# A two-layer diffusion transformer in split fp32 on one core: single chunk loads in the opening, one weighing step moved, and a new order at both joints of attention and MLP

## The chip, the core and the metric

The kernel runs on one core of one Trainium2 chip. A core has five engines that run side by side and are tied by semaphores: TensorE (PE in the profile) multiplies and transposes, VectorE (DVE), ScalarE (ACT) and GpSimd (POOL) work element by element, and SyncE (SP) issues most of the transfers from HBM. The metric is device time in microseconds, lower is better. Times in the profile count from the start of the span, that is from the first instruction of the profiled execution.

## The reference

One image (256 tokens, width 1024) and one context (256 tokens) go through two blocks. Each block scales and shifts its input by a vector made from a conditioning vector (`ada_w`), mixes the tokens, adds the gated result, normalises, and does the same with an MLP. The first block's mixer is a retention in both directions with 4 heads, the second's a neighbourhood attention with 32 heads. The second block needs no output for the context. Cut to what matters here:

```
for i in range(2):
    mod = silu_c @ ada_w[i] + ada_b[i]; mod_c = silu_cc @ ada_w[i] + ada_b[i]
    sh1, sc1, g1, sh2, sc2, g2 = split(mod, 6)            # the same for mod_c
    h, hc = x * (1 + sc1) + sh1, ctx * (1 + sc1c) + sh1c
    y, yc = (retention_mixer, neighbourhood_mixer)[i](h, hc, ...)
    x = layer_norm(ALPHA * x + g1 * y)
    h = x * (1 + sc2) + sh2
    x = layer_norm(ALPHA * x + g2 * (relu(h @ w1[i]) ** 2 @ w2[i]))
    # i == 0: the same two steps for ctx with mod_c and yc
return x
```

In the retention, `finish` normalises each head's output, multiplies it by `silu(g)` and projects it with `w_o`.

## The kernel before

**Split numbers.** All large products run on fp32 numbers split in two: a high part (a cast to fp32r on ScalarE, tile names that end in `hi` or `h`) and a low part (what is left, a subtraction on VectorE, `lo` or `l`). A product is three matmuls: high by high, high by low, low by high (`mm3`, which keeps the three together). So each weight tile goes through four steps: `fetch` has SP load it into one of four `raw` buffers (512 KB), ScalarE casts `hi`, `lows` has VectorE subtract `lo`, and TensorE uses both. The `raw` buffer is free again when `lo` is done. SP issues its loads in program order, and each waits until its buffer is free. `take(n, ahead, open_)` fetches up to `ahead` units, makes their low parts, and hands out the next n; with `open_` that many of the low parts may still be outstanding.

**Order.** An engine's instructions are put in order by a scheduler of the framework, except where a flag on the engine's wrapper (`InOrder`, whose call is L84, so that nearly all rows of the profile carry that line) keeps them in program order: `pe.on`, `act.on`, `dve.on`, `pool.on`. SP is always in program order. At the places of the change the flags are on: the order there is written by hand. Each engine works its queue strictly from the front, so an instruction that waits holds up all behind it.

**Opening.** The first modulation, the queries and the values of head 0 are computed in eight chunks of 128 of the 1024 input columns. For each chunk SP loads modulation weights (`rawq`, two transfers), the columns of x and context (into `R`), and the weights of Q and V (`raw`). Chunks 0 and 1 are loaded singly (`chunk_loads`), the others in pairs with rows twice as long (`pair_loads`). TensorE then does `chunk_sums` (32 small matmuls, `pada`), `chunk_turn` (transposes of the tokens, `pt`), `chunk_columns`, and with the modulated tokens (`hTh`, `hTl`) the products of the queries (`chunk_q`, into `pq`) and of the values (into `pv`: `part_v` by parts for chunks 0 and 1, `chunk_v` token block by token block for the rest). `first_columns` and `first_biases` transpose the conditioning vector and the bias rows, which come by ScalarE's queue. `turn_over(n)` puts n matmuls on a constant tile (`still`) into TensorE's queue; their result is not used.

**First head.** After the projections of K and the gates, `masked_scores`, four outputs `po` (normalised into `on` and `gs`) and two `gates` calls follow. `to_oT(t)` transposes `gs` (into `pT`) and splits it into `oh` and `ol`; `tok` multiplies these by `w_o`. For t = 2, 3 `gs` needs `sg`, the silu of the last gates. Beside that runs a background: `bg()` does one step of `bg_stream`, which loads 512 KB of later modulation weights (`rawa`, into the same four buffers) and weighs them: the first nine steps are matmuls for the gate rows, the following ones are VectorE work (`weigh`, four operations on `strips` a step, in order), and every step issues the load of the next one.

**First joint**, from the last head of the retention to the first layer's MLP: per token block t a normalisation (`stat`, `moments`, `white` with `shift_of`), transposes (`turn`), scale and shift (`affine`) and split (`mod_split`). The first two pairs of hidden blocks are computed for the latent tokens (`LAT`) while the context's blocks 2 and 3 are still on their way, and then for the context (`CTX`), into the other half of the same banks. `evac1` takes the square of the relu out of a bank (`relu_sq`: `r`, then `hid`). Before the context half all flags of `ORDER` go off.

**Second joint**, from the neighbourhood attention to the second MLP: `gather`, `attend`, `invert`, `flip` and `turned` are the steps of the last score blocks (the result goes into `oTh`, `oTl`), `wo_first` and `wo_last` the two halves of the output projection (`pnw`), `settle_last` adds them, `center` and `mod_pt` make the normalised tokens and their transposes, and `tok_part` does single parts of the first products of the MLP (`p1t`) for token blocks 0 and 1. `activate` and `turn_block` make the first hidden block of them. The loop over `f4` then does the other hidden blocks with `mm1` in the usual form; its first pass is the `opening`.

Of the kernel before, what the change touches and what calls it, by code (L numbers as in the profile page):

```python
# [17 lines left out]
P = 128  # L18
# [86 lines left out]
def kernel(  # L105
# [171 lines left out]
    def lows(n=100):  # L277
        for lo, raw, hi in pending[:n]:
            dve.tensor_sub(out=lo, in0=raw, in1=hi.bitcast(F32))
        del pending[:n]  # L280
# [66 lines left out]
    def ln_columns(rows):  # L347
# [9 lines left out]
        pool.dma_start(out=lns[:], in_=lsc[0:64, :P])  # L357

# [400 lines left out]
    def chunk_ada(k):  # L759

        raw = slot(AQ[k], [P, 2, KC, P], F32, "rawq")
# [5 lines left out]
    def pair_ada(k):  # L767

        raws = []
        for kh in range(2):  # L770
            raw = slot(AQ[k % 4 + kh], [P, 2, 4, 2 * P], F32, "rawq")
            for i in range(2):
                w_ap = ada_w[0][512 * kh : 512 * kh + 512, i * D + P * k : i * D + P * k + 2 * P]
                sp.dma_start(out=raw[:, i], in_=w_ap.rearrange("(k p) n -> p k n", p=P))
            raws.append(raw)
        for j in range(2):
            adas[k + j] = lambda i, kk, j=j: raws[kk // 4][:, i, kk % 4, tsl(j)]

    def chunk_x(k, n=1):
        cols = slice(P * k, P * (k + n))  # L780
# [28 lines left out]

    def pair_loads(k):  # L810
        pair_ada(k)
        chunk_x(k, 2)
        for j in range(2):
            ws[k + j] = Weights(k + j)

    still = scr("still", F32R)
    dve.memset(still[:].bitcast(F32), 1.0)
# [114 lines left out]
    def chunk_v(k, ts):  # L934
        w = ws[k]
        for t in ts:
            mm3(
                pv[t][:], hs(k, t * P, (t + 1) * P), (w.hi[:, w.V], w.lo[:, w.V]), k == 0, k == KC - 1
            )

    def part_v(k, a, b):
        w, h = (ws[k].hi, ws[k].lo), hs(k, 0, NT)
        for t in range(4):
            pe.matmul(
                pv[t][:], lhsT=h[a][:, tsl(t)], rhs=w[b][:, Weights.V],
                start=(k == 0 and a == b), stop=False,
            )
# [18 lines left out]
    turn_over(5)  # L966
# [9 lines left out]
    for k in range(KC):  # L976
# [6 lines left out]
        if k == 1:  # L983
# [3 lines left out]
        elif k:  # L987
            chunk_q(k)
        if k < KC - 1:
# [5 lines left out]
            if k > 1:  # L995
                ws[k + 1].low()
        if k in (0, 2):
            pair_loads(k + 4)
        if k > 1:
            chunk_v(k, (0, 1))  # L1000
        else:
            part_v(k, 1, 0)
        if k < KC - 1:
            chunk_columns(k + 1)
            chunk_modulate(k + 1, lambda: None if k > 1 else ws[k + 1].low())
        if k > 1:
            chunk_v(k, (2, 3))
        else:
            part_v(k, 0, 1)
# [62 lines left out]
    for h in range(RH):  # L1072
# [34 lines left out]
        def gates(ts, between=()):  # L1107

            pgs = [bank("pg") for _ in ts]
            for k in range(KC):  # L1110
# [3 lines left out]
                if h == 0 and k % 4 == 3 and (k < 4 or len(ts) > 1):  # L1114
# [56 lines left out]
        for t in range(4):  # L1171
# [14 lines left out]
            if t < 2:  # L1186
                pool.tensor_mul(out=gs[:, t, :], in0=on, in1=gs[:, t, :])

# [42 lines left out]
        else:  # L1231
# [14 lines left out]
            def white(t, mv, r):  # L1246
                act.activation(out=xns[t], in_=R[t], func=AF.Identity, scale=r[:], bias=shift_of(mv, r)[:])
# [18 lines left out]
            white(0, *m0)  # L1266
# [8 lines left out]
            white(1, *m1)  # L1275
# [12 lines left out]
            white(2, *m2)  # L1288
# [27 lines left out]

    G2 = None
    for hf in range(2):
# [9 lines left out]
        if hf == 0:  # L1328
            us = take(2, 2)
# [27 lines left out]
        for fp in range(len(hid), 8):  # L1357
# [3 lines left out]
            mm1(us, ALL, pb)  # L1361
            dve.on = hf == 0
# [544 lines left out]
    def wo_last(t, half, cols=slice(0, 512)):  # L1907
        ps = wops[half, t, cols.start] if half else bank("pnw")
        mmo(ps, t, (4, 5, 6, 7), us[2 * half : 2 * half + 2], cols, start=half == 0)
        return ps  # L1910
# [33 lines left out]
    lows(1)  # L1944
# [8 lines left out]
    us4 = take(2, 0)  # L1953
# [65 lines left out]
    lo0 = [affine_half(pts0, half, 0, True, (dve, pool)[half]) for half in range(2)]  # L2019
# [3 lines left out]
    lo0[0]()  # L2023
# [3 lines left out]
    fetch(2)  # L2027
    us4 += take(2, 0, 2)
    lo0[1]()
    mv1, r1 = moments(1)  # L2030
    p00, p01 = [bank("p1t") for _ in range(2)]
# [6 lines left out]
    tok_part(p00, 0, 0, *HL, HIGH)  # L2038
    tok_part(p00, 0, 0, *LH, LOW)
    tok_part(p01, 0, 1, *HH, start=True)  # L2040
    tok_part(p01, 0, 1, *LH, LOW)
    tok_part(p00, 0, 0, *LH, HIGH, stop=True)
# [181 lines left out]
```

## Time and profile before

| | |
|---|---|
| median of 3 runs | 1200.78 us (1199.64 to 1201.06) |
| profiled execution | 1201.29 us, of which its span 1199.5 us |
| mean granted clock of TensorE | 0.997 |
| busy share of TensorE, VectorE, ScalarE, GpSimd | 98%, 69%, 40%, 21% |
| traffic of the span | 193.16 MB, mean 161 GB/s |
| opening (chunks, until K of head 0) | 0 to 64.4 us |
| first head's outputs and gates | about 100 to 127 us |
| first joint | about 433 to 470 us |
| second joint | about 976 to 1052 us |

A row of the timeline gives start, length, engine, line, operation, output from inputs, shape and count, and in brackets how long the engine was idle before it and what ended that. A row of a window gives its length, then busy time and count of TensorE, its weight loads, VectorE, ScalarE and GpSimd, the granted clock, the share of the transfer engines and GB/s. Matmuls are pipelined: the length of one in the timeline is longer than the distance to the next one's start, and the distance is what counts.

### The profile page before, as it was taken

Reading aid. Unit: us, or ns where it says so; the run is one execution under the profiler, and the core shown is the slowest. Engines: PE = TensorE matmul, PEld = TensorE weight load, DVE = VectorE, ACT = ScalarE, POOL = GpSimd, SP = SyncE. Lnnn points to the kernel's source line nnn. Section 1 sums busy time; section 2 is a strip of 40 time slices with the busy share of each in tenths; the row PEclk is TensorE's granted clock in tenths of the full one; section 3 lists DMA queues with packets and bytes.
Section 4 is the critical chain, followed back from the end, with each engine's and each line's share of the span. In section 5 each row is a group of like instructions: output and inputs, shape, how many; then the busy total and the mean of one; then the engine's idle time right before and its main releaser. Section 6 shows DMA issues by size and latency. Waiting matters only on the chain.

```text
span 1199.5 us, 17825 instructions
## 1 busy us (share of the span) xinstructions
PE 1176.4 (98%) x6867; PEld 987.8 (82%) x6867; DVE 832.7 (69%) x1307; ACT 477.6 (40%) x809; POOL 250.9 (21%) x390
## 2 busy tenths in 40 slices
PE   7999999999999999999999999999999999999997
PEld 5777788888888889888888888889788878999886
DVE  3784976787688477668766675578577588787446
ACT  3561222323222246442212432237466665556341
POOL 1102500310330141582203000123343431000001
PEclk9999999999999999999999999999999999999999
DMA  9774543344345124866566665656344435566760
GB/s 304 222 230 126 158 157 105 106 141 141 96 150 152 59 71 141 243 120 199 172 184 203 210 198 192 193 154 201 86 139 126 114 122 155 175 212 204 234 209 37
DMA packets 130265, 193.16 MB, mean 161 GB/s; under 512 B 9676, under 2 KB 73332, under 8 KB 130180
## 3 DMA queue, kind: packets, MB, share of 16 engines
q1 hardware_dynamic: 121796, 179.02, 47.8%
q0 software_dynamic: 7232, 10.44, 4.1%
q10 hardware_dynamic: 1152, 2.56, 0.8%
q8 instruction: 54, 0.88, 0.3%
q14 instruction: 31, 0.25, 0.1%
HBM read 187.15 MB, written 5.75 MB: 161 GB/s over the span
## 4 chain that ended last, share of the span: by engine, by line
PE 87%; DVE 7%; DMA 2%; ACT 2%; issue 2%; POOL 1%; DVEq 0%; ACTq 0%; POOLq 0%; SPq 0%
PE p L84 40%; PE pq L84 7%; PE pv L84 7%; PE pg L84 7%; PE pw L84 6%; PE pn L84 5%; PE pnv L84 4%; PE po L84 2%; DVE lo L84 2%; PE pada L84 2%; PE ppt L84 2%; PE pS L84 1%; PE pqk L84 1%; PE pav L84 1%; DMA raw<-in_mlp_w_dram 1%
## 5 line engine op out<-in xcount | busy, mean ns | idle before, releaser
L84 ACT CAST hi<-raw 128x1024 fp32r<-128x1024 f32 (+2 forms) x228 | 231.7, 1032 | 316.5 <-PE p L84 117.7
L84 DVE TENSOR_TENSOR lo<-raw,hi 128x1024 fp32r<-128x1024 f32 (+2 forms) x228 | 277.3, 1229 | 100.7 <-ACT hi L84 100.3
L84 PE MATMUL p<-hi,hid 128*128 128x512 f32 (+1 forms) x832 | 241.6, 373 | 0.0
L84 PEld LDWEIGHTS p<-hi,hid 128*128 128x128 f32 x832 | 152.1, 188 | 27.7
L84 PE MATMUL p<-hTh,lo 128*128 128x256 f32 (+1 forms) x512 | 167.4, 327 | 3.0 <-DVE lo L84 3.0
L84 PE MATMUL p<-hTh,hi 128*128 128x256 f32 (+1 forms) x512 | 167.8, 328 | 0.2 <-ACT hTh L84 0.2
L84 PE MATMUL p<-hTl,hi 128*128 128x256 f32 (+1 forms) x512 | 167.2, 327 | 0.3 <-DVE hTl L84 0.3
L84 PE MATMUL p<-lo,hid 128*128 128x512 f32 (+1 forms) x416 | 155.2, 373 | 0.0
L84 DVE SCALAR_TENSOR_TENSOR acc<-rawa,scol,acc 128x1024 f32<-128x1024 f32 x56 | 74.7, 1344 | 65.5 <-DMA rawa<-in_ada_w_dram 65.5
L84 PEld LDWEIGHTS p<-hTh,lo 128*128 128x128 f32 x512 | 96.4, 188 | 12.3 <-DVE lo L84 3.6
L84 PEld LDWEIGHTS p<-hTl,hi 128*128 128x128 f32 x512 | 96.4, 188 | 9.4 <-DVE hTl L84 0.8
L84 PEld LDWEIGHTS p<-hTh,hi 128*128 128x128 f32 x512 | 96.3, 188 | 9.2 <-ACT hTh L84 0.4
L84 POOL TENSOR_TENSOR R<-R,acc 128x512 f32<-128x512 f32 x40 | 60.3, 1521 | 205.2 <-DVE acc L84 204.9
L84 PEld LDWEIGHTS p<-lo,hid 128*128 128x128 f32 x416 | 78.4, 188 | 13.6
L84 ACT CAST hid<-r 128x256 fp32r<-128x256 f32 (+1 forms) x64 | 32.0, 500 | 112.4 <-DVE r L84 112.4
L84 DVE SCALAR_TENSOR_TENSOR strips<-rawa,scol,strips 128x512 f32<-128x512 f32 x84 | 64.3, 822 | 0.0
L84 POOL TENSOR_TENSOR rstd<-rstd,misc 128x1 f32<-128x1 f32 x28 | 18.8, 672 | 209.4 <-DVE rstd L84 208.1
L84 ACT ACTIVATE s<-s,mn 128x512 f32<-128x512 f32 x64 | 45.5, 712 | 26.2 <-DVE mn L84 26.2
L84 PE MATMUL pw<-hi,oh 128*128 128x512 f32 x128 | 51.6, 403 | 0.0
L84 PE MATMUL pg<-hi,hTh 128*128 128x512 f32 x128 | 51.3, 401 | 0.0
L84 PE MATMUL pw<-hi,ol 128*128 128x512 f32 x128 | 50.5, 395 | 0.5 <-DVE ol L84 0.5
L84 DVE TENSOR_TENSOR hid<-r,hid 128x256 fp32r<-128x256 f32 (+1 forms) x64 | 34.5, 539 | 23.0 <-ACT hid L84 22.9
(238 smaller groups left out, 2308.9 us busy)
## 6 DMA issues: line engine op xcount, KB each, us to landing
raw<-in_mlp_w_dram SPq DMA_DIRECT2D x128, 512.0 KB, 4.6
rawa<-in_ada_w_dram SPq DMA_DIRECT2D x80, 512.0 KB, 3.9
raw<-in_ret_w_in_dram SPq DMA_DIRECT2D x42, 512.0 KB, 3.7
raw<-in_nat_w_in_dram SPq DMA_DIRECT2D x24, 512.0 KB, 5.0
rawq<-in_ada_w_dram SPq DMA_DIRECT2D x16, 512.0 KB, 6.6
raw<-in_ret_w_o_dram SPq DMA_DIRECT2D x16, 512.0 KB, 3.8
bias<-rpb_rows POOLq DMA_DIRECT2D x32, 128.0 KB, 2.9
raw<-in_nat_w_o_dram SPq DMA_DIRECT2D x8, 512.0 KB, 5.2
```

Of the source, the lines that this page charges most:

```text
L84: r = f(*args, **kwargs)
```

## The change

Four places change; the computation stays the same.

1. Opening: all chunks are loaded singly, four ahead (`pair_loads` is gone). All chunks run by parts: high by high first, then the high weights by the low tokens. Fillers: 16 ahead of everything, then 3, 1, 3 and 4 where there were 5 and 5. The sums of chunk 0 stand ahead of the bias transpose.
2. First head: after the first output, `bg_until(9)` and one more step of the background; in `gates` only the call at k = 3 is left.
3. First joint: a unit is fetched earlier, with its low part separately; the split of blocks 2 and 3 is made as high part now and low part later (`mod_high`); the context half of the first two pairs is done with all high by high products first (`ctx_mm1`), and TensorE keeps program order through it, until the first `mm1` of the following loop.
4. Second joint: `invert(n)` moves behind `attend(n - 1)`, a fetch in separate rows moves behind `attend(n)`, the last projection goes by parts (`wo_parts`), low parts of weights move between the steps, the low part of the tokens' second half goes from GpSimd to VectorE, the first parts of the MLP get a new order, and in the loop's opening one fetch and one low part follow each `relu_sq`.

```
+    def mod_high(tmp, half, t):
+        ks = slice(4 * half, 4 * half + 4)
+        raw, hi, lo = tmp[:].rearrange("p (k t) -> p k t", k=4), hTh[:, ks, tsl(t)], hTl[:, ks, tsl(t)]
+        act.copy(out=hi, in_=raw)
+        return lambda: dve.tensor_sub(out=lo, in0=raw, in1=hi.bitcast(F32))
...
-    for k in range(2):
+    for k in range(4):
         chunk_loads(k)
-    pair_loads(2)
     for e in (act, dve, pe):
         e.on = True
+    turn_over(16)
     first_columns()
+    turn_over(3)
+    chunk_sums(0, 0)
+    chunk_row(0, tsl(0))
+    turn_over(1)
     first_biases()
-    chunk_sums(0, 0)
-    turn_over(5)
-    chunk_row(0, tsl(0))
+    turn_over(3)
     chunk_sums(0, 1)
...
-    turn_over(5)
+    turn_over(4)
...
-        if k == 1:
+        if k:
             chunk_q(k, ((0, 0),))
             part_v(k, 0, 0)
             chunk_q(k, ((1, 0), (0, 1)))
-        elif k:
-            chunk_q(k)
...
-        if k in (0, 2):
-            pair_loads(k + 4)
-        if k > 1:
-            chunk_v(k, (0, 1))
-        else:
-            part_v(k, 1, 0)
+        if k < 4:
+            chunk_loads(k + 4)
+        part_v(k, 1, 0)
...
-                if h == 0 and k % 4 == 3 and (k < 4 or len(ts) > 1):
+                if h == 0 and k == 3:
                     bg(2 if G1s[0] is None else 1)
                     first_gate()
...
+            if h == 0 and t == 0:
+                bg_until(9)
+                first_gate()
+                bg()
...
+    def ctx_mm1(us, pb):
+        for i in range(2):
+            for k in (4, 5, 6, 7, 0, 1, 2, 3):
+                pe.matmul(
+                    pb[i][:, CTX], lhsT=us[k // 4][0][:, k % 4, tsl(i)], rhs=hTh[:, k, CTX],
+                    start=k == 4, stop=False,
+                )
+        for i in range(2):
+            for k in (4, 5, 6, 7, 0, 1, 2, 3):
+                wh, wl = (w[:, k % 4, tsl(i)] for w in us[k // 4])
+                pe.matmul(pb[i][:, CTX], lhsT=wl, rhs=hTh[:, k, CTX], start=False, stop=False)
+                pe.matmul(pb[i][:, CTX], lhsT=wh, rhs=hTl[:, k, CTX], start=False, stop=k == 3)
...
-            us = take(2, 2)
+            us = take(2, 2, 1)
...
             mm1(us, LAT, pbs[0], range(0, 4))
-            take(0, 1)
+            lows(1)
+            shift = shift_of(*m3)
             f2 = affine(2, turn(2))
-            white(3, *m3)
+            fetch(1)
+            low21 = mod_high(f2[1], 1, 2)
+            white(3, shift, m3[1])
+            low20 = mod_high(f2[0], 0, 2)
             mm1(us, LAT, pbs[0], range(4, KC))
+            lows(1)
+            low21()
             us += take(2, 2)
-            for half in range(2):
-                mod_split(f2[half], half, 2, dve)
             mm1(us[2:4], LAT, pbs[1], range(0, 4))
             p3 = turn(3)
             mm1(us[2:4], LAT, pbs[1], range(4, KC))
             f3 = affine(3, p3)
+            low20()
+            low31, low30 = (mod_high(f3[half], half, 3) for half in (1, 0))
+            low31()
+            low30()
             take(0, 1)
-            for half in range(2):
-                mod_split(f3[half], half, 3, dve)
             for fp in range(2):
                 evac1(pbs[fp], LAT, hts[fp])
-            for e in ORDER:
+            for e in ORDER[1:]:
                 e.on = False
             for fp in range(2):
-                mm1(us[2 * fp : 2 * fp + 2], CTX, pbs[fp])
+                ctx_mm1(us[2 * fp : 2 * fp + 2], pbs[fp])
                 evac1(pbs[fp], CTX, hts[fp])
...
             mm1(us, ALL, pb)
+            pe.on = False
...
-    add_to(1, 0, t01[0], dve)
-    invert(n)
     gather(n)
     attend(n - 1)
+    invert(n)
     flip(n)
     turned(n)
     lows(1)
+    add_to(1, 0, t01[0], dve)
     fetch(1, at=N_V)
-    lows(1)
-    fetch(1, True)
-
-    us = take(4, 0, 2)
+
+    us = take(2, 0)
...
     attend(n)
+    lows(1)
+    fetch(1, True)
     mmo(ps, 0, (6, 7), us[0:2], start=False, k0=4)
     lows(2)
+    us += take(2, 0)
+    settle_last(0, 0, ps)
     fetch(1)
-    settle_last(0, 0, ps)
-    lows(1)
-    settle_last(0, 1, wo_last(0, 1))
+    settle_last(0, 1, wo_parts(0, 1))
     mv0, r0 = moments(0)
     wo_first(1, 1, HALVES)
+    lows(1)
+    fetch(1)
...
-    lo0 = [affine_half(pts0, half, 0, True, (dve, pool)[half]) for half in range(2)]
+    lo0 = [affine_half(pts0, half, 0, True) for half in range(2)]
...
     mv1, r1 = moments(1)
+    lo0[0]()
...
     tok_part(p00, 0, 0, *HH, HIGH)
-    tok_part(p00, 0, 0, *HL, HIGH)
+    tok_part(p01, 0, 1, *HH, LOW, start=True)
+    tok_part(p01, 0, 1, *HH, HIGH)
     tok_part(p00, 0, 0, *LH, LOW)
...
             for i in range(2):
                 relu_sq(pb[i], LAT, ht[:, 2 * f2 + i, 0, :], ht[:, 2 * f2 + i, 1, :])
+                if opening:
+                    fetch(1)
+                    lows(1)
+                if opening and i == 0:
+                    turn_block(r10, 1, 0, hid[0])
+                    turn_block(r11, 1, 1, hid[0])
+            if opening:
+                for e in (pe, act, pool):
+                    e.on = False
```

More of the change, by code (lines that the diff above doesn't have):

```diff
@@ L275, in fetch, with lows @@
             units.append((hi, lo))
-    def lows(n=100):
+    def lows(n=100, eng=None):
         for lo, raw, hi in pending[:n]:
-            dve.tensor_sub(out=lo, in0=raw, in1=hi.bitcast(F32))
+            (eng or dve).tensor_sub(out=lo, in0=raw, in1=hi.bitcast(F32))
         del pending[:n]
@@ L759, in chunk_ada @@
     def chunk_ada(k):
-        raw = slot(AQ[k], [P, 2, KC, P], F32, "rawq")
+        raw = slot(AQ[k % 4], [P, 2, KC, P], F32, "rawq")
         for i in range(2):
@@ L765, in chunk_ada, with chunk_x @@
         adas[k] = lambda i, kk: raw[:, i, kk, :]
[L767 to L780, printed above, removed]
+    def chunk_x(k):
+        cols = tsl(k)
         for a, src in enumerate((x, ctx_in)):
@@ L945, in part_v @@
                 pv[t][:], lhsT=h[a][:, tsl(t)], rhs=w[b][:, Weights.V],
-                start=(k == 0 and a == b), stop=False,
+                start=(k == 0 and a == b), stop=(k == KC - 1 and b == 1),
             )
@@ L1244, in proj, with white @@
                 return gated(tok_mm(t, half, wus[half]), t, half, G1)
[L1246 to L1247 removed]
+            def white(t, shift, r):
+                act.activation(out=xns[t], in_=R[t], func=AF.Identity, scale=r[:], bias=shift[:])
             def turn(t):
@@ L1909, in wo_last, with wo_parts @@
         mmo(ps, t, (4, 5, 6, 7), us[2 * half : 2 * half + 2], cols, start=half == 0)
+        return ps
+    def wo_parts(t, half):
+        oTh, oTl = oTs[0]
+        ps = wops[half, t, 0]
+        for parts in (((0, 0), (1, 0)), ((0, 1),)):
+            for k in (4, 5, 6, 7):
+                w = us[2 * half + (k - 4) // 2]
+                for a, b in parts:
+                    pe.matmul(
+                        ps[:], lhsT=(oTh, oTl)[a][:, k, tsl(t)], rhs=w[b][:, k % 2, :],
+                        start=False, stop=k == 7 and b == 1,
+                    )
         return ps
@@ L1952 @@
     ht = slot(N_Q, [P, 4, 2, NLAT], F32R, "hid1")
-    us4 = take(2, 0)
+    us4 = take(2, 0, 1)
     def toks(t):
@@ L2026 @@
     stats[1] = st1
-    fetch(2)
-    us4 += take(2, 0, 2)
-    lo0[1]()
+    fetch(1)
+    us4 += take(2, 0, 3)
     mv1, r1 = moments(1)
+    lo0[0]()
     p00, p01 = [bank("p1t") for _ in range(2)]
@@ L2052 @@
     p10, p11 = [bank("p1t") for _ in range(2)]
-    tok_part(p10, 1, 0, *HH, start=True)
-    tok_part(p10, 1, 0, *HL)
+    tok_part(p10, 1, 0, *HH, LOW, start=True)
+    tok_part(p10, 1, 0, *HL, LOW)
+    tok_part(p10, 1, 0, *HH, HIGH)
+    tok_part(p10, 1, 0, *HL, HIGH)
+    tok_part(p01, 0, 1, *HL, LOW)
+    low1(1)
+    lows(1)
+    tok_part(p11, 1, 1, *HH, start=True)
+    tok_part(p10, 1, 0, *LH, HIGH)
     tok_part(p01, 0, 1, *HL, HIGH, stop=True)
-    low1(1)
     low1(0)
@@ L2086 @@
             mm1(us, LAT, pb, at=AT)
-            if opening:
-                turn_block(r10, 1, 0)
-                turn_block(r11, 1, 1)
-                for e in (pe, act, dve, pool):
-                    e.on = False
             dve.on = f4 < 3
```

42 lines of the change are left out of this document (13 added, 29 removed).

## The prediction

> **What bounds the kernel now.** I read the page first, then TensorE's waits over the whole span.
>
> ```profile
> span 1199.5 us, 17825 instructions
> PE 1176.4 (98%) x6867; PEld 987.8 (82%) x6867; DVE 832.7 (69%) x1307; ACT 477.6 (40%) x809; POOL 250.9 (21%) x390
> ...
> PE 87%; DVE 7%; DMA 2%; ACT 2%; issue 2%; POOL 1%; DVEq 0%; ACTq 0%; POOLq 0%; SPq 0%
> ```
>
> TensorE is busy for 98% and carries 87% of the chain that ends last. The diff leaves its real matmuls alone (it only reorders them and swaps ten filler ones for 27), so all that can be won is time in which TensorE waits, or runs at a lower clock. The waits name the places, and the diff touches each of them:
>
> ```profile
> PE p L84 <- DVE lo L84: 3.0, 3, 1.7
> PE pT L84 <- POOL gs L84: 1.9, 1, 1.9
> ...
> PE pt L84 <- DVE xn L84: 0.7, 1, 0.7
> PE pnw L84 <- ACT oTh L84: 0.5, 1, 0.5
> PE pt L84 <- DVE acol L84: 0.5, 1, 0.5
> ...
> PE pw L84 <- DVE ol L84: 0.5, 1, 0.5
> ```
>
> The opening is the fifth place. Its rows in the timeline (start, length, what ran, and in brackets the idle time before it) are:
>
> ```profile
> 4.73 0.25 PE L84 MATMUL pc<-cst,crow 16*128 16x16 f32 x1 [4.73 <-DMA cst<-in_consts_dram]
> 6.39 0.28 PE L84 MATMUL pc<-cst,brow 16*128 16x16 f32 x1 [1.41 <-DMA brow<-in_ada_b_dram]
> ...
> 7.62 1.44 PE L84 MATMUL pq<-still 128*128 128x256 f32 x5
> ...
> 12.89 1.05 PE L84 MATMUL pq<-hTh,hi 128*128 128x512 f32 x2
> 13.74 1.05 PE L84 MATMUL pq<-hTh,lo 128*128 128x512 f32 x2
> ...
> 16.38 1.08 PE L84 MATMUL pada<-rawq,cT 128*32 128x128 f32 x32
> ...
> 20.77 1.09 PE L84 MATMUL pv<-hi,hTh 128*128 128x512 f32 x4
> 21.70 0.62 PE L84 MATMUL pq<-hTh,lo 128*128 128x512 f32 x2
> 22.92 1.08 PE L84 MATMUL pada<-rawq,cT 128*32 128x128 f32 x32
> ...
> 54.86 1.08 PE L84 MATMUL pada<-rawq,cT 128*32 128x128 f32 x32
> ```
>
> Two things are to be seen. Nothing runs until the constants land at 4.7, and then the transpose of the bias rows holds the queue to 6.39. And two 512-wide matmuls need 13.74 − 12.89 = 0.85 us, 0.43 each, while at 20.77 four need 0.93, 0.23 each: the array starts at half speed. One chunk takes 22.92 − 16.38 = 6.54.
>
> **The change part by part.** All sums are on the profiled execution: 1201.29, a span of 1199.5 and 1.8 around it. The runs' median, 1200.78, is 0.5 lower, and I take that off at the end.
>
> *Opening.* Sixteen fillers (0.21 each at half speed, by the 0.43 above) take 3.4 us and fit into the 4.7 of waiting. The first sums of chunk 0 stand ahead of the bias transpose, so they start about 1.0 after the constants (silu and the copies of its columns lie between) instead of after 6.39: some 0.7 to 0.9 are won. The other eleven fillers, at full speed if the early ones have raised the clock, take 1.3; the ten of before took 2.7 (5 at 1.36, from 7.62 to the sums at 8.98, doubled): some 1.4 won. The first real products then start near 10.3 instead of 12.89, and run at 0.23 rather than 0.43, so that the ten wide ones between 12.89 and 16.38 (3.5 us) end near 12.8. There chunk 1's modulation weights decide. The traffic while these come in:
>
> ```profile
> 0.00:4.75 4.75, 0.02 (x1) 0.05 (x1) 0.54 (x2) 1.28 (x1) 0.43 (x6) 1.00 0.49 136
> 4.75:12.89 8.14, 6.73 (x52) 5.34 (x53) 2.19 (x10) 1.43 (x4) 0.00 (x0) 1.00 1.15 302
> ```
>
> A chunk is 1664 KB (1.70 MB); chunk 0 and chunk 1's 1.05 MB make 2.75 MB, of which 136 GB/s bring 0.65 by 4.75 and 302 GB/s the rest in 7.0: they land from 11.8 (transfers interleave, so perhaps 13). Sums of chunk 1 start at 13.0 instead of 16.38: 3.4 won. A single chunk takes 1.70 / 302 = 5.6 us, less than TensorE's 6.54, so single loads (six issues a chunk on SP, where a pair had ten for two) keep ahead. In the later chunks the order by parts costs nothing: the same matmuls, with two parts of the values between the modulation and the next use. The wait on acol (0.5) goes, as more work stands ahead of it; I set 0.2 against it for the high part now needed sooner. Together −3.9; bounds −2.5 (the sums of chunk 1 only start at 14.4) and −5.
>
> *First head.* A step of the weighing (four vector operations on the MLP's modulation) moves right behind the first output, and the next one to the first half of the last gates.
>
> ```profile
> L84 DVE SCALAR_TENSOR_TENSOR strips<-rawa,scol,strips x8: 740/744/1767, 110.5 to 129.5; 128x512 f32<-128x512 f32 x8
> L84 DVE TENSOR_SCALAR strips<-rawa,scol x2: 478/478/479, 109.7 to 110.1; 128x512 f32<-128x512 f32 x2
> ...
> 116.03 1.05 ACT L84 CAST hi<-raw 128x1024 fp32r<-128x1024 f32 x1 [3.77 <-DMA raw<-in_ret_w_o_dram]
> ...
> 116.48 0.39 PE L84 MATMUL pw<-hi,ol 128*128 128x512 f32 x1
> ...
> 117.76 1.05 ACT L84 CAST hi<-raw 128x1024 fp32r<-128x1024 f32 x1 [0.19 <-DMA raw<-in_ret_w_o_dram]
> ...
> 118.72 1.07 ACT L84 ACTIVATE sg<-pg 128x512 f32<-128x512 f32 x2
> ...
> 119.38 3.04 POOL L84 TENSOR_TENSOR gs<-sg,gs 128x512 f32<-128x512 f32 x2 [10.40 <-ACT sg L84]
> 120.78 0.90 PE L84 MATMUL pT<-cst,gs 128*128 128x128 f32 x4 [1.87 <-POOL gs L84]
> ```
>
> TensorE waits for gs, gs for sg, and sg stands on ScalarE behind two casts of weights whose raw buffers come free late. The moved step costs 2 × 0.48 + 2 × 0.74 = 2.4 us of VectorE, beside TensorE's work, and frees the first of the two buffers some 7 us earlier. But the next step (4 × 0.74 = 3.0, pinned in order) now stands ahead of both lo and both ol, and the last raw buffer is freed only behind it: by VectorE's order around 114.5, landing 118 to 119, the cast to 120, then sg; pT at 121.1 to 122, against 120.78. Queued behind that step on VectorE is ol, wanted by TensorE at 116.48 and ready about 117.4: 0.9 of a new wait, out of what follows. For this: the ol wait (0.5) after it goes. What the wait does to the clock:
>
> ```profile
> 117.63:121.05 3.42, 1.55 (x8) 1.00 0.44 129
> 121.05:124.46 3.41, 3.41 (x11) 0.50 0.07 24
> ```
>
> After a stretch of 3.42 us with 1.55 busy, the next was granted half, and cost 1.7. If two shorter waits replace one, that may go. I take −0.4, nearest to "as before"; bounds +1.5 (pT at 122, clock as before) and −4.5 (all of it gone).
>
> *First joint.* The three lo/hTl waits are gone early:
>
> ```profile
> 461.95 0.39 PE L84 MATMUL p<-hTh,lo 128*128 128x256 f32 x1 [0.76 <-DVE lo L84]
> ...
> 467.43 0.28 PE L84 MATMUL p<-hTh,hi 128*128 128x256 f32 x1
> ...
> 464.30 1.22 DVE L84 TENSOR_TENSOR lo<-raw,hi 128x1024 fp32r<-128x1024 f32 x1
> 465.43 1.29 DVE L84 TENSOR_TENSOR hTl<-aff,hTh 128x512 fp32r<-128x512 f32 x2
> 466.63 0.42 DVE L84 SCALAR_TENSOR_TENSOR r<-p,r 128x256 f32<-128x256 f32 x1
> ```
>
> But TensorE now keeps program order through the context half, whose first matmul writes a bank that r still reads. Before, out of order, it ran seven 512-wide matmuls of the next pair (7 × 0.23 = 1.6 us) ahead of the context half at 467.43. Now it ends the latent half near 463.6 and finds the context half blocked: on VectorE four aff (1.4), three hTl (2.0) and a lo (1.2) stand ahead of r, which ends near 466.6. TensorE idles 3.0 us and does what it had reached at 467.43 − 1.6 = 465.8 only at 466.6: +0.8, and +0.3 for the second r. The 2.9 gained in the waits is spent there. An idle of 3.0 in one stretch is more than the 1.9 that halved the clock at 121.05, so I add that row's 1.7: +2.8. Bounds 0 and +3.3.
>
> The Trainium skill's "TensorE: Matmul & The Clock Gate", section "HAM oscillation — how this bites in real kernels", asks only that no gap of TensorE exceed about 3.4 us; by it the 3.0 costs no clock, this joint +1.1, as in the first rival, and the total is 1.7 lower. The trace contradicts it with 1.87 us of idle time followed by half clock.
>
> *Second joint.* Here weights arrive late.
>
> ```profile
> 1003.56 0.57 POOL L84 TENSOR_TENSOR rstd<-rstd,misc 128x1 f32<-128x1 f32 x1 [12.36 <-DVE rstd L84]
> ...
> 1032.67 1.05 ACT L84 CAST hi<-raw 128x1024 fp32r<-128x1024 f32 x1 [1.58 <-DMA raw<-in_mlp_w_dram]
> ...
> 1036.91 0.38 PE L84 MATMUL p<-hTh,lo 128*128 128x256 f32 x1 [1.72 <-DVE lo L84]
> ...
> 1035.64 3.49 DVE L84 TENSOR_TENSOR lo<-raw,hi 128x1024 fp32r<-128x1024 f32 x3
> ```
>
> That lo was late because VectorE waited for a cast of hid that stood on ScalarE behind the raw landing at 1032.67, and then worked three lo off in one go. After the change one lo stands behind each relu step or half of the hidden block, and each frees a raw buffer for the next fetch. Adding the durations along VectorE's new order, the lo wanted at 1034.7 is done near 1030.3, its successor at 1033.1: the 1.7, and the third of the lo waits (0.5, some 14 us later), are gone, with their 0.2 each of restarting: −2.6. Earlier, oTh comes ahead of two lo (1.2 each) and its 0.5 goes; two parts of wo behind one another cover the lo. Yet lo now stands between rstd and nmr (VectorE at 1004.3 rather than POOL's 1004.1 sets it), so that the transposes of xn wait about 0.7: even. The second normalisation ends 2.2 us sooner, as hTl (POOL's half too, now VectorE's) moves behind it: its 0.7 goes, and 0.2 + 0.6 come back at the hTl parts. The product order hides the rest. −3.1; bounds +0.5 (a lo late in the new order by one cast) and −4.5.
>
> Sum: −3.9 − 0.4 + 2.8 − 3.1 = −4.6: 1196.7 on the profiled execution, **1196.2** by the median.
>
> **The rivals.**
> - *The clock holds and the first head's wait goes.* For it: idle times would straddle the 3.4 us stretches. Against: 1.87 was enough once. First joint +1.1, first head −2.1: −8.0, or 1192.8.
> - *The opening's gain is hidden anyway*: a later load sets the start of the first head. For it: 302 GB/s all the way to 22.92. Against: waits on DMA end at 6.39. Without the 3.9 less 0.5 for acol: 1199.6.
> - *Slower: single loads of 512-byte rows fall behind.* The point is 6.5 us a chunk; chunk 7's modulation weights follow six chunk times after chunk 0's load, which ends near 9.5. At 7.5 us (227 GB/s) they land at 9.5 + 45 + 4.6 = 59, where TensorE wants them at 54.86 − 3.4, or 51.5: the opening ends about 8 later than planned, +3.9 instead of −3.9: 1204. Against it: 302 GB/s with chunks 0 and 1 loaded singly.
>
> **How the numbers follow.** The forecast gets 0.55, the first rival 0.17, the second 0.15, the third 0.13. Its own range: half of each part's distance to its bounds, added as squares, is 2.6 down (0.6, 2.1, 1.4, 0.7) and 2.2 up (0.7, 1.0, 0.3, 1.8), so 1193.6 to 1198.4. For 8 in 10 I reach to 1190.5 (first rival with more of the second joint) and 1202.5 (most of the second, the edge of the third). No change is within 0.2%, ±2.4 us, about what a measurement of this kernel can tell. Faster takes 0.85 of the forecast, all of the first rival and a quarter of the second: 0.68; slower nearly all of the third: 0.12; same 0.20.
>
> **What would show it.** Opening: sums of chunk 1 at about 13.0, the eight starts 6.3 to 6.6 apart. First head: pT still waiting 1 to 2 us for gs, ol newly for lo. First joint: one wait of about 3 us for r at 460 on TensorE's clock, with half clock behind it. Second: no wait over 0.5 for lo after 1025. Wrong if chunks' starts drift apart beyond 6.6, if no wait for r appears, or if lo waits stay.

## The result, and the profile after

| | before | after |
|---|---|---|
| median of 6 runs each | 1200.75 us (1199.64 to 1201.65) | 1194.6 us (1193.21 to 1197.68) |
| ratio of times | | 0.9949, 95% interval 0.9939 to 0.9959 |
| profiled execution, its span | 1201.29, 1199.5 | 1193.21, 1191.4 |

The change saves 6.15 us by the medians, 0.5%, and the interval lies wholly below 1: a small gain, but clear of the noise. The forecast was 4.6 (1196.2). The profiled execution after is the fastest of its six, and saves 8.1. Its mean granted clock is 0.998, that of the other five 0.996 or 0.997; only the profiled one has a trace, so where the others lost their time is not shown.

The page of the kernel after, its first lines and the shares of the chain that ended last:

```profile
span 1191.4 us, 17865 instructions
PE 1175.3 (99%) x6884; PEld 987.6 (83%) x6884; DVE 833.5 (70%) x1308; ACT 479.4 (40%) x809; POOL 246.7 (21%) x389
...
PE 92%; DVE 3%; ACT 2%; issue 2%; POOL 1%; DMA 0%; DVEq 0%; POOLq 0%; ACTq 0%
```

TensorE's share of the chain went from 87% to 92%, VectorE's fell from 7% to 3%, DMA's from 2% to nothing. TensorE's waits in the kernel after (released by, in total, times, longest):

```profile
PE p L84 <- DVE r L84: 2.4, 1, 2.4
PE pT L84 <- POOL gs L84: 1.5, 1, 1.5
PE pq L84 <- DVE still L84: 1.2, 1, 1.2
PE pw L84 <- DVE ol L84: 0.8, 1, 0.8
PE pt L84 <- ACT xn L84: 0.6, 1, 0.6
```

The waits for lo, xn from VectorE, oTh and acol are gone. The longest one now, r, did not stand there before.

Where the 8.1 us came from is read by laying the starts of the same TensorE instruction in both profiles beside each other:

| first instruction of | before | after | ahead by | since the row above |
|---|---|---|---|---|
| sums of chunk 1 (`pada`) | 16.38 | 12.92 | 3.46 | 3.46 |
| masked scores of head 0 (`pS`, high by low) | 84.57 | 80.64 | 3.93 | 0.47 |
| `pT` of head 1 | 217.12 | 211.56 | 5.56 | 1.63 |
| first layer's second product (`p` from `hid`) | 542.66 | 537.86 | 4.80 | −0.76 |
| first parts of the second MLP (`p1t`) | 1009.25 | 1004.35 | 4.90 | 0.10 |
| last product | 1191.36 | 1183.64 | 7.72 | 2.82 |

The remaining 0.37 lies in the tail. So: opening 3.9, first head 1.6, first joint −0.8, second joint 2.9.

**Opening.** TensorE's timeline of the kernel after:

```profile
1.23 3.78 PE L84 MATMUL pq<-still 128*128 128x256 f32 x16 [1.23 <-DVE still L84]
5.00 0.25 PE L84 MATMUL pc<-cst,crow 16*128 16x16 f32 x1
...
5.92 0.65 PE L84 MATMUL pada<-rawq,cT 128*32 128x128 f32 x16
...
10.45 0.70 PE L84 MATMUL pq<-hTh,hi 128*128 128x512 f32 x2 [0.35 <-ACT hTh L84]
10.99 0.63 PE L84 MATMUL pq<-hTh,lo 128*128 128x512 f32 x2
11.45 1.08 PE L84 MATMUL pv<-hi,hTh 128*128 128x512 f32 x4
...
12.92 1.08 PE L84 MATMUL pada<-rawq,cT 128*32 128x128 f32 x32
...
19.47 1.16 PE L84 MATMUL pada<-rawq,cT 128*32 128x128 f32 x32
```

The sixteen fillers fill the wait for the constants. Two wide matmuls from 10.99 to 11.45 take 0.23 each, where the same two took 0.43. The first period of a chunk, 19.47 − 12.92 = 6.55, is that of before (6.54), with single loads; the later ones are 6.70, 6.55, 6.34, 6.35 and 6.94. No wait of TensorE for a transfer stands among them.

**First head.** ScalarE, GpSimd and TensorE in the kernel after:

```profile
114.05 1.05 ACT L84 CAST hi<-raw 128x1024 fp32r<-128x1024 f32 x1 [3.93 <-DMA raw<-in_ret_w_o_dram]
115.00 1.08 ACT L84 ACTIVATE sg<-pg 128x512 f32<-128x512 f32 x2
...
115.68 3.06 POOL L84 TENSOR_TENSOR gs<-sg,gs 128x512 f32<-128x512 f32 x2 [8.82 <-ACT sg L84]
...
113.48 0.50 PE L84 MATMUL pw<-hi,ol 128*128 128x512 f32 x1 [0.76 <-DVE ol L84]
117.53 0.66 PE L84 MATMUL pT<-cst,gs 128*128 128x128 f32 x4 [1.47 <-POOL gs L84]
```

`sg` still stands behind the cast of a late weight tile, and `ol` is late as well, just as the order of VectorE had it.

**First joint.** TensorE and VectorE in the kernel after:

```profile
457.94 0.28 PE L84 MATMUL p<-hTh,lo 128*128 128x256 f32 x1
460.67 0.39 PE L84 MATMUL p<-hTh,hi 128*128 128x256 f32 x1 [2.45 <-DVE r L84]
...
457.59 1.29 DVE L84 TENSOR_TENSOR hTl<-aff,hTh 128x512 fp32r<-128x512 f32 x2 [0.56 <-ACT hTh L84]
459.06 1.23 DVE L84 TENSOR_TENSOR lo<-raw,hi 128x1024 fp32r<-128x1024 f32 x1 [0.17 <-ACT hi L84]
460.20 0.42 DVE L84 SCALAR_TENSOR_TENSOR r<-p,r 128x256 f32<-128x256 f32 x1
```

The latent half ends at 458, the context half can start at 460.67: between them TensorE has nothing it is allowed to do.

**Second joint.** In the kernel after, TensorE waits once for xn; on VectorE the low parts come singly or in twos, and none of TensorE's waits behind 1017 reaches 0.2:

```profile
1000.54 1.09 PE L84 MATMUL pt<-cst,xn 128*128 128x128 f32 x8 [0.55 <-ACT xn L84]
...
1024.80 1.23 DVE L84 TENSOR_TENSOR lo<-raw,hi 128x1024 fp32r<-128x1024 f32 x1 [0.52 <-ACT hi L84]
...
1028.45 2.36 DVE L84 TENSOR_TENSOR lo<-raw,hi 128x1024 fp32r<-128x1024 f32 x2 [0.53 <-ACT hi L84]
```

### The profile page after: what moved, and what is told of

Read it like the earlier page. It is cut to its first block, busy times and chain, and to the rows that moved or that the text cites. A ratio compares the mean times of both kernels' runs of the same rounds, so it can differ in the third digit from the quotient of the medians.

```text
span 1191.4 us, 17865 instructions
## 1 busy us (share of the span) xinstructions
PE 1175.3 (99%) x6884; PEld 987.6 (83%) x6884; DVE 833.5 (70%) x1308; ACT 479.4 (40%) x809; POOL 246.7 (21%) x389
## 4 chain that ended last, share of the span: by engine, by line
PE 92%; DVE 3%; ACT 2%; issue 2%; POOL 1%; DMA 0%; DVEq 0%; POOLq 0%; ACTq 0%
PE p L84 43%; PE pq L84 8%; PE pv L84 7%; PE pw L84 7%; PE pg L84 7%; PE pn L84 5%; PE pnv L84 4%; PE po L84 2%; PE pada L84 2%; PE pS L84 1%; PE ppt L84 1%; PE pqk L84 1%; PE pav L84 1%; PE pt L84 1%; ACT s L84 1%
## 5 line engine op out<-in xcount | busy, mean ns | idle before, releaser
L84 ACT CAST hi<-raw 128x1024 fp32r<-128x1024 f32 (+2 forms) x228 | 232.6, 1033 | 323.7 <-PE p L84 117.7
L84 PE MATMUL p<-hTh,hi 128*128 128x256 f32 (+1 forms) x512 | 163.2, 328 | 2.5 <-DVE r L84 2.4
L84 DVE SCALAR_TENSOR_TENSOR strips<-rawa,scol,strips 128x512 f32<-128x512 f32 x84 | 61.4, 786 | 0.0
L84 PE MATMUL pg<-hi,hTl 128*128 128x512 f32 x128 | 50.0, 390 | 0.0
```

Source lines behind the costliest of these rows:

```text
L84: r = f(*args, **kwargs)
```

## The experiments

Every kernel was timed beside the kernel before on the same chip. In the three groups below the kernel before had medians of 1202.07 (single parts), 1201.57 (`evac_early`, `step_late`, `ctx_warm`, `best`) and 1201.52 (the others); so ratios are compared across groups, not times.

### The four parts, one at a time

Each kernel is the kernel before with one of the four parts of the diff alone.

> Theory (the prediction's steps): the opening is worth its 3.9 us wherever it stands, since nothing between it and the first joint waits for a load. The kernel before with the new opening alone: -3.9 us, about 1196.8; first sums of chunk 1 at 12.9, starts of chunks 6.3 to 6.7 apart, and the wait of pT for gs as before (1.9 us). Rival (a later load sets the start of the first head): within 1 us of before; the masked scores start at 84.6 as before.

Measured: 1196.73 us against 1202.07, ratio 0.9966 (0.9953 to 0.9979), that is −4.1. Sums of chunk 1 started at 13.08, the masked scores at 80.66, 3.91 ahead of before, so the opening is worth its 3.9 by itself and the rival fell. Two details were off: the last spacing of chunks is 6.97, and `pT` waited 2.34 for gs, not 1.9.

> Theory: the wait moves rather than goes: a wait of ol of about 0.8 us stands newly at 116.5, pT still waits 1.5 us for gs, and the stretch at half clock behind it comes or not with the execution; between -0.3 and -2.0 us, about 1199.5. Rival (the moved step frees the buffer and the wait ends): pT without a wait, -4 us.

Measured: 1200.63 us, ratio 0.9993 (0.9984 to 1.0002), −0.8. `ol` waited 0.8, `pT` 2.0. The wait moved, as expected; by the timing this part alone cannot be told from no change.

The traces tell more. From the masked scores to `pT` of head 1 the profiles of the kernels that share one of the two orders took (us, with the kernel):

| order of the first head | no stretch at half clock there | one stretch at half clock there |
|---|---|---|
| as before | 132.37 (`second_joint_alone`), 132.38 (`open_alone`) | 132.55 (before), 132.21 (`first_joint_alone`) |
| as after | 130.92 (after) to 131.46 (`weigh_alone`), six profiles | 132.88 (`no_first_joint`) |

So the new order is worth 0.9 to 1.5 us without any help of the clock, and in the old order the half clock cost next to nothing. TensorE in `second_joint_alone`, with the old first head and the full clock:

```profile
121.14 0.66 PE L84 MATMUL pT<-cst,gs 128*128 128x128 f32 x4 [2.36 <-POOL gs L84]
...
126.86 0.50 PE L84 MATMUL pw<-hi,ol 128*128 128x512 f32 x1 [1.41 <-DVE ol L84]
```

The wait for `ol` is 1.41 here and was 0.45 in the kernel before: a TensorE at half speed lost time there that it would have waited anyway.

> Theory: this part costs time by itself: TensorE, held in program order, waits 2.4 us for r ahead of the context half where it waited 1.5 us in three places and did later work ahead; +0.8 to +1.1 us, about 1201.7, and +1.7 more in executions in which the clock goes to half behind it. Rival: it gains the three waits it removes, -1.5 us or more.

Measured: 1202.94 us, ratio 1.0015 (1.0003 to 1.0027), +1.8: this part alone makes the kernel slower, by little, with the interval just above 1. Its profiled execution had the half clock. Windows of that kernel, TensorE alone (length, busy time and count, granted clock, share of the transfer engines, GB/s):

```profile
463.03:466.45 3.42, 1.11 (x10) 1.00 0.20 70
466.45:469.87 3.42, 3.27 (x15) 0.50 0.51 153
```

A stretch in which TensorE was busy for 1.11 of 3.42 us, and the next one at half clock. From the first product of the layer to the second this kernel took 94.19 us, the kernel before 92.28.

> Theory: the two waits for lo at the opening of the MLP (1.7 and 0.5 us) and the wait for xn go, small waits come back: -2.9 us, about 1197.9. Rival: the gain needs the earlier parts (other times of the loads), then less than 1.5 us.

Measured: 1199.83 us, ratio 0.9989 (0.9978 to 1.0001), −1.3 by the ratio, though 2.2 by the medians and 2.9 by the spans of the profiled executions (1196.6 against 1199.5). In the trace the part did what was expected: the two waits for lo (1.72 and 0.53 us, ending at 1036.91 and 1049.96 in the kernel before) and the one for oTh are gone. The timing alone leaves it open.

### What the parts wait for

**Relu steps early.** The kernel after with

```
             p3 = turn(3)
+            evac1(pbs[0], LAT, hts[0])
             mm1(us[2:4], LAT, pbs[1], range(4, KC))
...
-            for fp in range(2):
-                evac1(pbs[fp], LAT, hts[fp])
+            evac1(pbs[1], LAT, hts[1])
```

> The changed kernel, with the relu steps of the first pair of hidden blocks (r, hid) ahead of the scale and shift of block 3. Theory: the first joint's wait of 2.4 us comes from r standing behind four aff, three hTl and a lo on VectorE; moved ahead, r is done before TensorE ends the latent half, and the wait falls below 1 us (then for hTh or hTl): 1.4 to 2.2 us less than the changed kernel, about -7.9 us against before, and no half clock at the joint. Rival (the context half waits for its own tokens hTh as long): wait of 2 us or more for hTh, same time as the changed kernel.

Measured: 1193.07 us, ratio 0.9931 (0.9914 to 0.9947), −8.3; the interval overlaps that of the kernel after, so by the timing alone the gain over it is not settled. The joint's wait in this kernel:

```profile
459.31 2.22 PE L84 MATMUL p<-hTh,hi 128*128 128x256 f32 x16 [1.04 <-ACT hTh L84]
```

2.45 for r became 1.04 for hTh, and the second product of the first layer started at 536.28, 1.6 ahead of the kernel after with the opening and the first head at the same times to 0.1. So r was late for its place in VectorE's queue. What is left is the price: r and hid now stand ahead of the scale and shift of block 3, which hTh needs. In the profiled execution a wait of 1.1 for a lo at 780.8 took most of it back. The kernel `step_out` (below) had that wait too, 1.13 at 778.15; `best`, with the same joint, and `step_late` did not. What brings it is open.

**Weighing step late.** The kernel after with

```
-                if h == 0 and k == 3:
+                if h == 0 and k == (3 if len(ts) == 1 else 7):
```

> The changed kernel, with the second weighing step behind the two splits of oT instead of ahead of them. Theory: that step holds both ol (new wait of 0.8 us) and the raw buffer of the last projection weights, whose cast stands ahead of sg (wait of 1.5 us); behind them, both waits go: 2.0 to 2.5 us less than the changed kernel, about -8.3 us against before. Rival (sg is late for another reason, GpSimd's 1.5 us an operation): pT still waits over 1 us.

Measured: 1196.08 us, ratio 0.9954 (0.994 to 0.9967), −5.5: no better than the kernel after. The theory fell in part. TensorE's waits at the first head of this kernel:

```profile
116.41 0.65 PE L84 MATMUL pT<-cst,gs 128*128 128x128 f32 x4 [1.11 <-POOL gs L84]
...
122.31 0.50 PE L84 MATMUL pw<-hi,ol 128*128 128x512 f32 x1 [1.60 <-DVE ol L84]
```

`pT` came 1.1 earlier and the first ol wait went; but the step, four operations of 1.05 with GpSimd busy beside it, now stood ahead of the third ol, which then was 1.6 late. The wait only went further back.

**Fillers in the joint's wait.** The kernel after with

```
+            pw = bank("warm")
+            for _ in range(20):
+                pe.matmul(pw[:, :256], lhsT=hTh[:, 0, tsl(0)], rhs=hTh[:, 0, LAT], start=True, stop=True)
             for fp in range(2):
                 ctx_mm1(us[2 * fp : 2 * fp + 2], pbs[fp])
```

> The changed kernel, with 20 filler matmuls (2.4 us, results unused) in TensorE's wait for r at the first joint. Theory of the clock: the idle stretch of 2.4 us costs a stretch at half clock (1.7 us) in part of the executions; filled, it never does: median 0 to 1.7 us lower than the changed kernel, and no half clock between 455 and 470 us. Rival: the clock does not fall for 2.4 us of idle time, then no gain, or some tenths lost because the fillers end late.

Measured: 1193.9 us, ratio 0.9938 (0.9924 to 0.9953), −1.3 against the kernel after by the ratios, but the intervals overlap: unclear. No wait for r is left in the trace, and no half clock at the joint. But the profile of the kernel after had no half clock there either, and from the first product to the second both took 93.0 us. So no trace shows what the fillers save.

**Both moves.** The edits of the relu steps and of the late weighing step together.

> Both moves together (relu steps early, second weighing step late). Theory: the two are 340 us apart and add: 3.5 to 4.7 us less than the changed kernel, about 1190 to 1191 where before has 1200.8 (-10 us). Rival: the second joint or the loads take part of it back: -8 us.

Measured: 1192.58 us, ratio 0.9927 (0.9912 to 0.9941), −8.8; the interval just reaches into that of the kernel after. The late step gave nothing again (ol waited 1.6).

**Weighing step out of the gates, relu steps early.**

```
-                if h == 0 and k == 3:
+                if h == 0 and k == 3 and len(ts) == 1:
```

> The changed kernel with relu steps early, and with the second weighing step taken out of the last gates, so that it stands behind all four splits of oT. Theory: with that step behind ol for t = 2, 3 as well, no wait of ol is left (0.8 us in the changed kernel at t = 0, 1.6 us with the step late at t = 2), and pT waits about 1.1 us for GpSimd alone: first head 1.2 to 2.0 us shorter than in the changed kernel, the whole 2.6 to 3.6 us faster than it, near -9.5 us against before. Rival: the raw buffer that the step holds longer starves the next head's weights, and a wait for hi or lo near 125 us takes it back.

Measured: 1190.33 us, ratio 0.9912 (0.9897 to 0.9926), −10.6. Its interval lies wholly below that of the kernel after: of the versions run this is the fastest. At the first head TensorE waits for nothing:

```profile
115.03 0.40 PE L84 MATMUL pw<-hi,ol 128*128 128x512 f32 x1
115.26 0.60 PE L84 MATMUL pT<-cst,gs 128*128 128x128 f32 x4
115.62 0.48 PE L84 MATMUL pw<-hi,oh 128*128 128x512 f32 x1
```

VectorE's queue in this kernel shows why: the step begins at 120.30, behind the last of the four ol.

```profile
116.88 0.68 DVE L84 TENSOR_TENSOR ol<-pT,oh 128x512 fp32r<-128x512 f32 x1
...
119.69 0.69 DVE L84 TENSOR_TENSOR ol<-pT,oh 128x512 fp32r<-128x512 f32 x1 [0.36 <-ACT oh L84]
120.30 2.93 DVE L84 SCALAR_TENSOR_TENSOR strips<-rawa,scol,strips 128x512 f32<-128x512 f32 x4
```

From the masked scores to head 1's `pT` it was 2.8 us faster than the kernel after, more than expected: the wait for GpSimd's gs went too. With the step out of the way VectorE made the low parts of the weights earlier (from 108.25 rather than 110.47), and `sg` started at 112.05 rather than 115.00. The rival's shortage of weights near 125 did not come.

**No fillers in the opening.** The kernel after without the line `turn_over(16)`.

> The changed kernel without the 16 fillers ahead of the first transpose. Theory: they raise the clock at about 5.4 us; without them it rises one to three stretches of 3.4 us later, and the sums, fillers and first products run at half speed: first sums of chunk 1 at 14 to 15 instead of 12.9, 1 to 2 us slower than the changed kernel. Rival: chunk 1's loads set that start anyway (12.9 as before): no difference.

Measured: 1197.06 us, ratio 0.9962 (0.9949 to 0.9976), some 1.5 us slower than the kernel after by the ratios, whose intervals overlap a little, and 3.9 by the spans of the profiled executions. TensorE in this kernel:

```profile
12.26 1.19 PE L84 MATMUL pq<-hTh,hi 128*128 128x512 f32 x2
13.25 1.05 PE L84 MATMUL pq<-hTh,lo 128*128 128x512 f32 x2
14.11 1.91 PE L84 MATMUL pv<-hi,hTh 128*128 128x512 f32 x4
15.81 0.71 PE L84 MATMUL pq<-hTl,hi 128*128 128x512 f32 x2
16.45 1.08 PE L84 MATMUL pada<-rawq,cT 128*32 128x128 f32 x32
```

Sums of chunk 1 start at 16.45, as before the change (16.38), though those of chunk 0 started at 5.83: two wide matmuls from 13.25 take 0.43 each, half clock up to 16. More than expected hangs on the fillers: without them the masked scores start at 84.02, with them at 80.64, before the change at 84.57.

An early clock alone is not enough either. `second_joint_alone` has the opening of before, and in its profile the full speed came earlier than in that of the kernel before: two wide matmuls from 12.89 take 0.23 each. TensorE there:

```profile
14.84 1.08 PE L84 MATMUL pada<-rawq,cT 128*32 128x128 f32 x32
...
22.52 0.43 PE L84 MATMUL pada<-rawq,cT 128*32 128x128 f32 x8 [0.27 <-DMA rawq<-in_ada_w_dram]
23.27 0.44 PE L84 MATMUL pt<-cst,R 128*128 128x128 f32 x2 [0.33 <-DMA R<-in_x_dram]
24.02 0.44 PE L84 MATMUL pada<-cst,R 128*128 128x128 f32 x2 [0.31 <-DMA R<-in_ctx_dram]
```

Chunk 1 starts at 14.84, 1.54 ahead of the kernel before; then TensorE waits for the loads of the first pair, chunk 3 is only 0.14 ahead and the masked scores 0.13. So the gain of the opening needs both: fillers that bring the full speed early, and loads that are there by then. It rests on one profile, with the full speed later than in the kernel after.

**First joint as before.** The kernel after with this part of the diff undone.

> The changed kernel with the first joint of before. Theory: the first joint costs 0.75 us in an execution without half clock and 2.5 with one: 0.7 to 2 us faster than the changed kernel, -7 to -8 us against before, and no wait for r. Rival: the new joint gains with the new opening: slower than the changed kernel.

Measured: 1195.93 us (1193.66 to 1199.24), ratio 0.9953 (0.9938 to 0.9969): not told apart from the kernel after. In the traces the joint is 0.74 shorter (447.69 to 539.99 against 444.82 to 537.86, from the first product to the second), as expected; but this profiled execution lost 0.9 us in the opening, 2.0 at the first head, where it had a stretch at half clock, and some 3 in the second MLP, of which below. The timing is inconclusive.

**Loop's opening as before.** The kernel after with the last hunk of the diff undone.

> The changed kernel, with the loop's opening of the second MLP as before (two relu steps in one go, no fetch and no low part between them, turned blocks ahead of them). Theory: the last lo waits (1.7 and 0.5 us) went by this interleaving, so about 2 us of the second joint's 2.9 come back, with a wait for lo of over 1 us after 1025 us. Rival: the earlier fetches and the order of the low parts ahead of the loop removed them; then under 0.7 us comes back.

Measured: 1197.3 us, ratio 0.9965 (0.9953 to 0.9976), some 1.9 slower than the kernel after, with intervals that overlap a little. In the trace 1.24 of it lies behind 1018. VectorE and TensorE there:

```profile
1030.28 3.49 DVE L84 TENSOR_TENSOR lo<-raw,hi 128x1024 fp32r<-128x1024 f32 x3
...
1031.56 0.38 PE L84 MATMUL p<-hTh,lo 128*128 128x256 f32 x1 [0.49 <-DVE lo L84]
```

The three lo in one go are back (3.49, as before), and the wait, but 0.49 where it was 1.72. Between theory and rival: by the traces the interleaving is worth 1.1 to 1.2 of the 2.9, the order ahead of the loop the rest.

## Why the prediction was right, point by point

- *Bound.* TensorE's matmuls hold the span; gains came only from its waits and its clock. Right: busy time 1176.4 and 1175.3, and the span 8.1 shorter.
- *Opening, −3.9.* Measured −3.9, sums of chunk 1 at 12.92 for a forecast of 13.0, chunk period 6.55. That the sum fits to a tenth is luck in part: its terms as written (3.4, 0.5 for acol, 0.2 against) make 3.7. They were mixed up too: I counted 0.7 to 0.9 for the bias transpose's new place and held chunk 1's loads for the limit. Without the early fillers the sums of chunk 0 come early just the same and the opening wins 0.5 in all (84.02 against 84.57). So the gain hangs on the full speed, reached at about 5 rather than 15, together with loads that are there by then: with the loads in pairs an earlier full speed won 0.13. My sign of being wrong, spacings beyond 6.6, appeared (6.70 and 6.94 in the kernel after), but with no wait for a transfer: it was set too tight. In the longer one a transpose waits 0.46 for `pv` (at 49.82); what makes the 6.70 is open (6.55 in `open_alone`).
- *First head, −0.4.* Measured −1.6 in the profile. Every wait came as the order said: ol 0.76 (forecast 0.9), cast at 114.05 (118 less the 3.9 of the opening), pT 1.47. The size was off, and not for the clock: I priced the half clock behind the wait at 1.7, but in the old order it cost 0.2 at most (132.55 and 132.21 with it, 132.37 and 132.38 without). What went are waits: 2.36 and 1.41 in the old order at full clock, 1.47 and 0.76 after. In the new order a stretch at half clock does cost 1.4 to 2.0 (`no_first_joint`), and here none came, which is luck of the execution. Alone, this part measured −0.8.
- *First joint, +2.8.* The mechanism was right, and it is the sharpest test: a new wait, for r, of 2.45 (forecast 3.0). The sum +1.1 without the clock measured +0.76. The waits that went were 0.76, 0.24 and 0.35, 1.35 together and not 2.9 as I wrote; the sum did not use that number. The half clock came in the profiles of this part alone and of `step_late`, where it cost 1.2 and 1.5 rather than 1.7 (94.19 and 94.53 us from product to product, 93.04 after), and did not come in that of the kernel after. It is a price that some executions pay, and I charged it in full. This term, 2.0 too high, and the first head's, 1.2 too small, make up most of the 3.5 us between the forecast 4.6 and the 8.1 of the profiled execution. How the 1.6 between forecast and median divides is not shown, as the median execution has no trace.
- *Second joint, −3.1.* Measured −2.9. As forecast no wait for lo or oTh is left; xn waits 0.55 (forecast 0.7), and 0.2 for hTh and 0.33 for hTl came back (forecast 0.2 and 0.6).
- *Rivals.* The first, 1192.8, is close to the profiled execution (1193.21), and its condition on the clock held. But the first head's wait, which it lets go, stayed (1.47 and 0.76), so it is near for partly other reasons. The median lies between it and the forecast. The second fell: the opening's 3.9 arrived at the masked scores (80.64 against 84.57). The slower one fell too: in eight of the ten profiles with the new opening TensorE waited nowhere over 0.21 between chunk 1 and chunk 6. The loads are not far from the limit, though: in `step_out` chunk 2's sums waited 0.42 for `rawq`, and in `no_first_joint` TensorE stood 0.98 at 37.50 behind Q and V weights that landed late (their cast had waited 2.27 for the load).
- *The Trainium skill's* "HAM oscillation" section of "TensorE: Matmul & The Clock Gate" would have no loss of clock below 3.4 us of idle time. The runs contradict it: 2.45 us were enough in two of the five profiles that had this wait.

## What to carry to other kernels

A wait that a reordering removes is gained only if what stands next in the same queue is early too: list, for each engine, what the moved instruction now stands ahead of. An off-path step belongs behind the last instruction that the path waits for, not merely behind the first: late was worth nothing here, out of the way some 2.8 us. And while a first transfer is on its way, cheap matmuls ahead of it can bring the full speed early, which is worth as much as the loads behind it can follow: 3.4 us here with single loads, 0.13 in a profile with pairs. A stretch at half clock must be priced by what comes next: it cost up to 2.0 us where TensorE set the pace, and next to nothing where TensorE would have waited for VectorE anyway.

## What the runs showed of the hardware

**Two waits of the same length, with and without half clock.** In every profile the changes of the granted clock lie a whole number of 3.41 us apart, with a start that differs by execution. What the profiles point to is TensorE's busy time within one such stretch. Two stretches of one and the same wait, in the kernel after and in `step_late`, each with the next one where it changed:

```profile
455.97:459.38 3.41, 2.25 (x19) 2.05 (x18) 2.68 (x6) 3.30 (x7) 0.00 (x0) 1.00 0.43 142
459.38:462.79 3.41, 2.10 (x15) 1.90 (x16) 2.47 (x6) 1.38 (x4) 0.00 (x0) 1.00 0.34 105
462.79:466.20 3.41, 3.41 (x31) 3.41 (x30) 1.90 (x5) 1.74 (x5) 0.53 (x1) 1.00 0.14 49
```

```profile
459.73:463.15 3.42, 1.75 (x12) 1.00 0.24 67
463.15:466.56 3.41, 3.41 (x18) 0.50 0.25 87
```

In the kernel after the wait of 2.45 us straddles the edge at 459.38 and leaves both stretches busy for 2.1 or more: full clock. In `step_late` 1.65 of it falls into one, busy for 1.75: half. The same wait straddles an edge in `no_fill` and `no_interleave` (no half clock) and falls mostly into one stretch in `first_joint_alone` (1.11 busy, half clock). Over all profiles, between the start and the tail, stretches with 1.11, 1.32, 1.52, 1.55 and 1.75 busy were followed by half clock, but others with 1.60, 1.63, 1.75, 1.78 and 1.79 were not, nor any with 1.82 or more (the ends of matmuls are modelled). So between about 1.6 and 1.8 busy time alone does not tell which comes, and whether a wait of 1.5 to 2.5 us is followed by half clock differs from execution to execution.

**The same matmuls at two speeds at full clock.** In the profiled execution of `no_first_joint` the second MLP's first products, 256 wide, started 117.7 ns apart, in all other profiles mostly 113.3. Windows of the kernel after, and of `no_first_joint`:

```profile
1030.00:1070.00 40.00, 40.00 (x355) 40.00 (x354) 34.45 (x51) 25.82 (x46) 0.00 (x0) 1.00 0.67 211
```

```profile
1030.00:1070.00 40.00, 40.00 (x342) 40.00 (x342) 33.42 (x49) 25.43 (x44) 0.00 (x0) 1.00 0.65 202
```

355 matmuls in 40 us against 342, TensorE busy throughout and the clock granted in full; over the 768 of that product it makes about 3 us. What causes it stays open. It showed in one of fourteen profiles; whether it is a part of the 4 to 5 us by which executions of one kernel differ here is not shown.
